# The last down projection of a two-layer diffusion backbone: its first two groups are loaded and split within the last up block, later weights load later, and the last four row tiles go in the order 0, 2, 1, 3

## The chip, the cores and the metric

The kernel runs on one core of a Trainium2 chip. The metric is device time in microseconds, from one launch to its end. A core has five engines that work side by side, each on a list of instructions of its own: PE (TensorE, matrix products), DVE (VectorE), ACT (ScalarE), POOL (GpSimd) and SP (SyncE, which here only issues transfers). PEld is PE's loading of a weight tile.

## The reference

Two layers over 1024 latent tokens of width 1024 and 256 context tokens. Each layer has a token mixer and then a gated feed-forward network with a convolution over positions. The change touches only the very last matrix product, `@ w_down` of the second layer:

```python
def conv_ffn(h, w_up, conv_w, conv_b, w_down):
    a, b = jnp.split(h @ w_up, 2, axis=-1)
    ap = jnp.pad(a, ((0, 0), (1, 1), (0, 0)))
    a = ap[:, :-2] * conv_w[0] + ap[:, 1:-1] * conv_w[1] + ap[:, 2:] * conv_w[2] + conv_b
    return (jax.nn.gelu(a) * b) @ w_down
...
x = x + g2 * rms_norm(conv_ffn(h, f_w_up[i], f_conv_w[i], f_conv_b[i], f_w_down[i]), norm_g[i, 3])
```

The hidden width is 2816, which is 22 blocks of 128. In the second layer only the latent tokens are needed, and `x` is the output.

## The kernel before

**Exact products from split numbers.** Each float32 operand is split in two: ACT casts it to a high part (`CAST`, tiles `ah` and `wh`), DVE subtracts to get the low part (`TENSOR_TENSOR`, tiles `al` and `wl`). A product is three matmuls: high by high, high by low, low by high. `split_into` does one split, so each 128x1024 operand costs one cast on ACT and one subtraction on DVE before PE can use it.

**The up projection.** `lat_ffn` walks over the 22 blocks of the hidden width. `up` makes one block with seven block products (a fast-multiplication scheme in the style of Strassen and Winograd) in the accumulators X, Y, Z (`psB`). Their weights come from the generator `weights`, advanced by `step(more)` inside the block before. The tiles `wh` and `wl` have four buffers each, and a block uses all four. `conv_gate` makes the gated activations, and `Q.dma_start(actd[...])` on SP writes them to memory (`actd`). `pair_sums` reads two blocks back and writes four combinations (`actc`).

**The down projection.** `down_blocks` does the same trick for the 1024x2816 by 2816x1024 product: seven products `p1`, `p6`, `p7`, `p4`, `p5`, `p3`, `p2`, each over 11 pairs of blocks, taken two pairs at a time as groups 0 to 5 (group 5 has one pair). A group is 24 matmuls (12 for group 5), so a product is 132. `fetch(p, g)` loads the activations (tile `raw`) and what it needs of the weights, and splits both. It runs up to three groups ahead of the matmuls. The weights come as four quarters: `r1` (quarter 11), `r12`, `r22`, and quarter 21, which is loaded where it is used. `p1` needs `r1` alone. `p6` needs `r12 - r1` (written over `r1`) and `r22` minus that. Before the change `fetch("p1", g)` loads `r1[g]`, `r12[g]` and, for the first three groups, `r22[g]`, each as two transfers of 256 KB on SP.

**The accumulators.** `p1` and `p2` accumulate in two tiles `psA` of two banks each: row tiles 0 and 1 share the first, 2 and 3 the second. After `p1`, ACT copies the four banks to `s1` (`after("p1")`). The products `p6`, `p7`, `p4` go to four `psB` tiles. At the end, the last three groups of `p2` are done row tile by row tile (15 matmuls each), and `final(t)` squares, gates, normalises, adds and stores that row tile.

**The order of the work.** The code's order is a wish: a scheduler in the framework places instructions by its own costs, and each engine then runs its list as it stands. A wait on a tile is a wait on the whole tile, both banks of a `psA` included. In the trace nearly all instructions carry L50, a helper's line, so they are told apart by their tiles.

Of the kernel before, what the change touches and what calls it, by code (L numbers as in the profile page):

```python
# [15 lines left out]
P = 128  # L16
# [16 lines left out]
def hybrid_kernel(  # L33
# [24 lines left out]
    Q = Engine(nc.sync, "Q")  # L58
# [32 lines left out]
    def t_row(dt=F32, shape=(P, 1024)):  # L91
        return sb.tile(list(shape), dt, name=nm("row"), tag="row", bufs=10)
# [848 lines left out]
    def lat_ffn(l, stage, n0, halos, gate, between, steady, ctx=None, after=None):  # L941
# [98 lines left out]
        def pair_sums(n, f0, f1):  # L1040
# [16 lines left out]
            yield  # L1057

        def run_late():
            while late:  # L1060
                late.pop(0)()

        def next_weights(nxt):
            W = ahead.pop("W")
            if nxt is None:
                return W, iter(())
            ahead["W"] = {}
            return W, weights(l, nxt[0], ahead["W"], nxt[1] in ("plain", "ctx"))
# [135 lines left out]
        for (f, how), nxt in zip(jobs, jobs[1:] + [None]):  # L1204
# [10 lines left out]
            n = made.index(f)  # L1215
# [4 lines left out]
        if ctx is None:  # L1220
            step(sums_, 9)
            down_blocks(l, stage, gate, pairs, pair_sums(len(pairs) - 1, *pairs[-1]))
            return
# [84 lines left out]

    def down_blocks(l, stage, gate, pairs, rest):
        open_pool("down%d" % l)  # L1310
# [8 lines left out]
        def kept(tag, n=1024):  # L1319
            return pool.tile([P, n], F32, name=nm(tag), tag=tag, bufs=1)  # L1320

        first = [(a_tile("h"), a_tile("l")) for _ in range(3)]
        r1 = [kept("r1%d" % g) for g in range(NG)]
        r12 = [kept("r12%d" % g) for g in range(NG)]
        ys = [kept("y%d" % t) for t in range(8)]
        s1 = [kept("s1%d" % i, n=512) for i in range(4)]
        r22 = [t_row() for _ in range(NG)]

# [4 lines left out]

        sides = {"p1": (0, 0), "p2": (1, 0), "p4": (1, 512)}
        kinds = {"p5": 0, "p6": 1, "p7": 2, "p3": 3}
        ready = {}

        def fetch(p, g):
            n = width[g]
            raw = t_raw()  # L1340
            if p in kinds:
                a = members[g][0]
                Q.dma_start(raw[:, 0:n].rearrange("p (k c) -> p k c", c=512),
                            actc[kinds[p], a:a + len(members[g])].rearrange("k p c -> p k c"))
            else:
                second, o = sides[p]
                for j, m in enumerate(members[g]):
                    Q.dma_start(raw[:, j * 512:(j + 1) * 512], actd[pairs[m][second], :, o:o + 512])
            if p == "p1":
                w_part(r1[g], g, 0, 0)  # L1350
                w_part(r12[g], g, 0, 1)
                if g < 3:
                    w_part(r22[g], g, 1, 1)
                src = r1[g]
            elif p == "p6":
                if g < 3:
                    w_part(r22[g + 3], g + 3, 1, 1)
                V.tensor_sub(r1[g][:, 0:n], r12[g][:, 0:n], r1[g][:, 0:n])
# [9 lines left out]
            else:  # L1368
                src = t_raw()
                w_part(src, g, 1, 0)  # L1370
                if p == "p4":
                    V.tensor_sub(src[:, 0:n], src[:, 0:n], r22[g][:, 0:n])
                    V.tensor_tensor(out=src[:, 0:n], in0=src[:, 0:n], in1=r1[g][:, 0:n], op=ALU.add)
            ops = []
            for x, tiles in ((raw, first.pop(0) if first else [a_tile(z) for z in "hl"]),
                             (src, [t_w("w" + z) for z in "hl"])):
                split_into([t[:, 0:n] for t in tiles], x[:, 0:n])
                ops.append(tiles)
            ready[p, g] = ops

# [105 lines left out]
        while got < len(todo):  # L1486
            fetch(*todo[got])
            got += 1
        for i in range(4):
            while chores:  # L1490
                chores.pop(0)()
            for p, g in tail:
                mms(A[i], p, g, list(range(len(members[g]))), i, False, g == NG - 1)
            final(i, A[i])
# [572 lines left out]
```

## Time and profile before

| what | value |
|---|---|
| median of 3 runs | 2918.66 us (2913.76 to 2921.04) |
| profiled execution, its own time | 2913.42 us |
| its span, first to last instruction | 2911.6 us |
| PE busy | 2775.0 us, 95% of the span |
| DVE, ACT, POOL busy | 72%, 47%, 23% |
| mean granted TensorE clock | 0.984 |
| transfers | 513.78 MB, mean 176 GB/s |

Times in the rows below are microseconds from the span's start. In a timeline a row is: start, duration, engine, line, operation, output tile <- inputs, shape, how many were merged; in brackets the idle time of that engine just before, and what ended it. In the chain of waits a row is: start, length, engine or transfer, and the chain follows from the last instruction back to whatever released it. In a table by stretch a row gives busy time and, after it, the granted clock, the share of DMA engines busy and GB/s.

### The profile page before, as it was taken

What the parts mean: (1) busy time and instruction counts of PE and PEld (TensorE: products, weight loads), DVE (VectorE), ACT (ScalarE), POOL (GpSimd) and SP (SyncE); (2) the same over time, 40 slices, a digit from 0 to 9 for tenths busy, and PEclk for the clock granted to TensorE, in tenths of its full rate; (3) what the DMA queues carried; (4) which work ended last, traced back from release to release, by engine and by line L of the source; (5) the groups of instructions that cost most, each with busy time, mean ns of one, the idle gap of its engine ahead of it and who ended that gap; (6) DMA issues with size and microseconds to landing.
All of it is one profiled execution on the core that took longest, in us unless ns stands there. A gap on an engine that the chain in (4) does not pass through costs nothing.

```text
span 2911.6 us, 40240 instructions
## 1 busy us (share of the span) xinstructions
PE 2775.0 (95%) x14702; PEld 2387.4 (82%) x14702; DVE 2108.0 (72%) x3175; ACT 1371.2 (47%) x2298; POOL 677.2 (23%) x1002
## 2 busy tenths in 40 slices
PE   7999999999999999999999999899997999999998
PEld 5798988999898888888877777888886988887787
DVE  6557675655787888778643669887886688887766
ACT  4332242323575445544324534777875444444433
POOL 1150130620201122220003025565552112220001
PEclk9999999999999999999999999999997999999999
DMA  7764356522575323546855865356575345445654
GB/s 258 238 193 147 115 176 217 170 89 80 191 231 176 112 98 121 161 159 213 298 168 175 280 206 185 113 172 228 184 237 178 116 156 184 149 145 182 231 170 156
DMA packets 418200, 513.78 MB, mean 176 GB/s; under 512 B 18641, under 2 KB 298065, under 8 KB 418001
## 3 DMA queue, kind: packets, MB, share of 16 engines
q1 hardware_dynamic: 361585, 448.01, 48.1%
q10 hardware_dynamic: 55264, 58.99, 6.0%
q0 software_dynamic: 1152, 4.19, 0.4%
q8 instruction: 116, 1.90, 0.3%
q14 instruction: 83, 0.68, 0.1%
HBM read 403.12 MB, written 108.00 MB: 176 GB/s over the span
## 4 chain that ended last, share of the span: by engine, by line
PE 50%; DMA 9%; DVE 6%; ACT 3%; issue 3%; POOL 2%; SPq 0%; ACTq 0%; DVEq 0%; POOLq 0%
PE psB L50 42%; PE psA L50 8%; DVE row L50 2%; DVE wl L50 2%; DMA raw<-in_f_w_up_dram 2%; DMA raw<-in_f_w_down_dram 2%; DMA raw<-actd 1%; ACT wh L50 1%; ACT row L50 1%; ACT tmp L50 1%; POOL sm L50 1%; DMA row<-xT 1%; DMA araw<-in_ada_w_dram 0%; DMA raw<-in_ada_w_dram 0%; ACT act L50 0%
## 5 line engine op out<-in xcount | busy, mean ns | idle before, releaser
L50 PE MATMUL psB<-cmb,wh 128*128 128x512 f32 (+2 forms) x2584 | 748.5, 374 | 4.7 <-ACT row L50 2.4
L50 ACT CAST wh<-raw 128x1024 fp32r<-128x1024 f32 (+1 forms) x376 | 331.8, 895 | 481.2 <-PE psB L50 177.9
L50 PEld LDWEIGHTS psB<-cmb,wh 128*128 128x128 f32 x2584 | 471.9, 188 | 94.1 <-ACT row L50 3.3
L50 PE MATMUL psB<-cmb,wl 128*128 128x512 f32 (+2 forms) x1292 | 482.8, 374 | 0.0
L50 DVE TENSOR_TENSOR wl<-raw,wh 128x1024 fp32r<-128x1024 f32 (+1 forms) x376 | 382.6, 1030 | 115.2 <-ACT wh L50 114.4
L50 PE MATMUL psB<-wh,big 128*128 128x512 f32 x864 | 285.8, 398 | 3.4 <-DVE row L50 2.0
L50 PEld LDWEIGHTS psB<-cmb,wl 128*128 128x128 f32 x1292 | 243.3, 188 | 43.4
L50 POOL TENSOR_SCALAR sm<-sm 128x1 f32<-128x1 f32 (+1 forms) x76 | 42.9, 565 | 938.6 <-ACT junk L50 382.1
L50 POOL TENSOR_TENSOR row<-raw,raw 128x512 f32<-128x512 f32 x44 | 74.9, 1702 | 593.9 <-DMA raw<-in_f_w_up_dram 435.1
L50 ACT CAST wh<-row 128x512 fp32r<-128x512 f32 (+1 forms) x150 | 118.1, 789 | 179.0 <-DVE row L50 93.7
L50 PE MATMUL psB<-wh,act 128*128 128x512 f32 x640 | 199.8, 390 | 1.6 <-DVE tmp L50 1.6
L50 PE MATMUL psA<-big,wh 128*128 128x320 f32 x1024 | 194.5, 312 | 2.9 <-ACT wh L50 1.7
L50 PEld LDWEIGHTS psB<-wh,big 128*128 128x128 f32 x864 | 163.9, 190 | 40.6 <-ACT big L50 2.4
L50 DVE SCALAR_TENSOR_TENSOR row<-row,cwcols,row 128x1024 f32<-128x1024 f32 (+2 forms) x142 | 151.0, 1064 | 37.2 <-ACT row L50 21.8
L50 ACT CAST ah<-raw 128x1024 fp32r<-128x1024 f32 (+1 forms) x79 | 79.7, 1011 | 198.2 <-PE psB L50 111.5
L50 PE MATMUL psB<-wl,big 128*128 128x512 f32 x432 | 167.3, 396 | 0.0
L50 PEld LDWEIGHTS psA<-big,wh 128*128 128x128 f32 x1024 | 160.8, 189 | 3.9 <-ACT wh L50 2.3
L50 DVE TENSOR_TENSOR al<-raw,ah 128x1024 fp32r<-128x1024 f32 (+1 forms) x79 | 92.6, 1174 | 95.0 <-ACT ah L50 94.8
L50 POOL TENSOR_SCALAR row<-row,sm,sm 128x128 f32<-128x128 f32 x160 | 120.9, 770 | 148.5 <-DMA row<-vscr 142.5
L50 PE MATMUL psB<-wh,al 128*128 128x512 f32 x388 | 151.2, 390 | 0.0
L50 PE MATMUL psB<-wh,ah 128*128 128x512 f32 x388 | 151.1, 390 | 0.0
L50 PE MATMUL psB<-wl,ah 128*128 128x512 f32 x388 | 151.1, 389 | 0.0
(275 smaller groups left out, 6212.0 us busy)
## 6 DMA issues: line engine op xcount, KB each, us to landing
raw<-in_f_w_up_dram SPq DMA_DIRECT2D x142, 512.0 KB, 4.7
raw<-in_a_w_in_dram SPq DMA_DIRECT2D x64, 512.0 KB, 4.8
raw<-in_ada_w_dram SPq DMA_DIRECT2D x64, 512.0 KB, 4.8
wh<-woscr SPq DMA_DIRECT2D x48, 512.0 KB, 4.7
raw<-actd SPq DMA_DIRECT2D x44, 512.0 KB, 4.7
actd<-row SPq DMA_DIRECT2D x39, 512.0 KB, 2.6
raw<-in_a_w_out_dram SPq DMA_DIRECT2D x35, 512.0 KB, 3.5
xT<-row ACTq DMA_DIRECT2D x33, 512.0 KB, 5.1
```

The lines of the kernel that those rows point to most:

```text
L50: ins = fn(*a, **kw)
```

## The change

It does four things.

- A generator `lead_in` runs within the last up block, where there are no more up weights to prepare. It loads the activations and the `r1` weights of groups 0 and 1 of `p1` (into tiles `raw` and `row`) and splits them into `wh` and `wl` tiles as these come free. `down_blocks` then takes them as ready, and the three early `a` tiles serve groups 2, 3 and 4.
- `r12` and `r22` are no longer loaded with `fetch("p1", g)`, but by a table `side_loads`, partly with the later groups of `p1` and partly with those of `p6`. The number of bytes stays the same.
- `r1[0]`, `r1[1]` live in `row` tiles and `r22[0]`, `r22[1]` in the stage's own pool, the other way round than before.
- The last four row tiles are taken in the order 0, 2, 1, 3 instead of 0, 1, 2, 3.

```diff
--- before.py
+++ after.py
@@ -1056,6 +1056,35 @@
             Q.dma_start(actc[2:4, n].rearrange("s p c -> p s c"), w.rearrange("p (s c) -> p s c", s=2))
             yield
 
+        early = {}
+
+        def lead_in():
+            def load(n):
+                raw = t_raw()
+                for j in range(2):
+                    Q.dma_start(raw[:, j * 512:(j + 1) * 512], actd[pairs[2 * n + j][0], :, 0:512])
+                return raw
+
+            def halves(src):
+                hl = [t_w("w" + z) for z in "hl"]
+                split_into(hl, src)
+                return hl
+
+            acts, early["b11"] = [], [t_row(), t_row()]
+            for n, w in enumerate(early["b11"]):
+                acts.append(load(n))
+                for j in range(2):
+                    f = pairs[2 * n + j][0]
+                    Q.dma_start(w[:, j * 512:(j + 1) * 512], w_down[l][f * P:(f + 1) * P, 0:512])
+            yield
+            early["act"] = [halves(acts[0])]
+            yield
+            early["w"] = [halves(early["b11"][0])]
+            yield
+            yield
+            early["act"].append(halves(acts[1]))
+            early["w"].append(halves(early["b11"][1]))
+
         def run_late():
             while late:
                 late.pop(0)()
@@ -1063,7 +1092,7 @@
         def next_weights(nxt):
             W = ahead.pop("W")
             if nxt is None:
-                return W, iter(())
+                return W, lead_in() if ctx is None else iter(())
             ahead["W"] = {}
             return W, weights(l, nxt[0], ahead["W"], nxt[1] in ("plain", "ctx"))
 
@@ -1219,7 +1248,7 @@
         run_late()
         if ctx is None:
             step(sums_, 9)
-            down_blocks(l, stage, gate, pairs, pair_sums(len(pairs) - 1, *pairs[-1]))
+            down_blocks(l, stage, gate, pairs, pair_sums(len(pairs) - 1, *pairs[-1]), early)
             return
         open_pool("down%d" % l)
         pool = stage_pool["pool"]
@@ -1306,7 +1335,7 @@
             step(extra, 99)
             ctx_down(l, stage, gate, chain(*[ada_cols(1, m, st, accs, True) for m, st, accs in sums]), after)
 
-    def down_blocks(l, stage, gate, pairs, rest):
+    def down_blocks(l, stage, gate, pairs, rest, early):
         open_pool("down%d" % l)
         pool = stage_pool["pool"]
         NP = len(pairs)
@@ -1320,11 +1349,11 @@
             return pool.tile([P, n], F32, name=nm(tag), tag=tag, bufs=1)
 
         first = [(a_tile("h"), a_tile("l")) for _ in range(3)]
-        r1 = [kept("r1%d" % g) for g in range(NG)]
+        r1 = early["b11"] + [kept("r1%d" % g) for g in range(2, NG)]
         r12 = [kept("r12%d" % g) for g in range(NG)]
         ys = [kept("y%d" % t) for t in range(8)]
         s1 = [kept("s1%d" % i, n=512) for i in range(4)]
-        r22 = [t_row() for _ in range(NG)]
+        r22 = [kept("r22%d" % g) for g in range(2)] + [t_row() for _ in range(2, NG)]
 
         def w_part(dst, g, second, h):
             for j, m in enumerate(members[g]):
@@ -1332,13 +1361,18 @@
                 Q.dma_start(dst[:, j * 512:(j + 1) * 512], w_down[l][f * P:(f + 1) * P, h * 512:(h + 1) * 512])
 
         sides = {"p1": (0, 0), "p2": (1, 0), "p4": (1, 512)}
+        side_loads = {("p1", 2): ((0, 0),), ("p1", 3): ((0, 1), (1, 0)), ("p1", 4): ((0, 2),), ("p1", 5): ((0, 3), (1, 1)),
+                      ("p6", 0): ((0, 4), (1, 2)), ("p6", 1): ((0, 5), (1, 3)), ("p6", 2): ((1, 4),), ("p6", 3): ((1, 5),)}
         kinds = {"p5": 0, "p6": 1, "p7": 2, "p3": 3}
         ready = {}
 
         def fetch(p, g):
             n = width[g]
-            raw = t_raw()
-            if p in kinds:
+            hl = early["act"][g] if p == "p1" and g < 2 else None
+            raw = None if hl else t_raw()
+            if hl:
+                pass
+            elif p in kinds:
                 a = members[g][0]
                 Q.dma_start(raw[:, 0:n].rearrange("p (k c) -> p k c", c=512),
                             actc[kinds[p], a:a + len(members[g])].rearrange("k p c -> p k c"))
@@ -1346,15 +1380,13 @@
                 second, o = sides[p]
                 for j, m in enumerate(members[g]):
                     Q.dma_start(raw[:, j * 512:(j + 1) * 512], actd[pairs[m][second], :, o:o + 512])
+            if p == "p1" and g > 1:
+                w_part(r1[g], g, 0, 0)
+            for second, m in side_loads.get((p, g), ()):
+                w_part((r12, r22)[second][m], m, second, 1)
             if p == "p1":
-                w_part(r1[g], g, 0, 0)
-                w_part(r12[g], g, 0, 1)
-                if g < 3:
-                    w_part(r22[g], g, 1, 1)
                 src = r1[g]
             elif p == "p6":
-                if g < 3:
-                    w_part(r22[g + 3], g + 3, 1, 1)
                 V.tensor_sub(r1[g][:, 0:n], r12[g][:, 0:n], r1[g][:, 0:n])
                 src = t_row()
                 V.tensor_sub(src[:, 0:n], r22[g][:, 0:n], r1[g][:, 0:n])
@@ -1371,12 +1403,15 @@
                 if p == "p4":
                     V.tensor_sub(src[:, 0:n], src[:, 0:n], r22[g][:, 0:n])
                     V.tensor_tensor(out=src[:, 0:n], in0=src[:, 0:n], in1=r1[g][:, 0:n], op=ALU.add)
-            ops = []
-            for x, tiles in ((raw, first.pop(0) if first else [a_tile(z) for z in "hl"]),
-                             (src, [t_w("w" + z) for z in "hl"])):
-                split_into([t[:, 0:n] for t in tiles], x[:, 0:n])
-                ops.append(tiles)
-            ready[p, g] = ops
+            if hl is None:
+                hl = first.pop(0) if first else [a_tile(z) for z in "hl"]
+                split_into([t[:, 0:n] for t in hl], raw[:, 0:n])
+            if p == "p1" and g < 2:
+                wl = early["w"][g]
+            else:
+                wl = [t_w("w" + z) for z in "hl"]
+                split_into([t[:, 0:n] for t in wl], src[:, 0:n])
+            ready[p, g] = hl, wl
 
         def mms(bank, p, g, js, i, first, last):
             (ah, al), (wh, wl) = ready[p, g]
@@ -1486,7 +1521,7 @@
         while got < len(todo):
             fetch(*todo[got])
             got += 1
-        for i in range(4):
+        for i in (0, 2, 1, 3):
             while chores:
                 chores.pop(0)()
             for p, g in tail:
```

How this moves instructions at three places:

**ACT, from the end of the last up block through p1.** `row_24825`/`row_24841` is the block's last copied accumulator. `r_4252` to `r_4254` are the weights `r1` of groups 0 to 2 before. After the change `row_24749`/`row_24750` are those of groups 0 and 1, and `r_4264` those of group 2. Before:

```order
L50 COPY row_24775<-psB_24747 128x2x256
L50 COPY row_24825<-psB_24746 128x2x256
L50 ACTIVATE row_24859<-row_24825,lncols,cwcols_734 128x1024
L50 CAST ah_24875<-raw_24913 128x1024
L50 CAST ah_24877<-raw_24928 128x1024
L50 CAST ah_24879<-raw_24943 128x1024
L50 CAST wh_24922<-r_4252_24881 128x1024
L50 ACTIVATE row_24859<-row_24859 128x1024
L50 CAST wh_24937<-r_4253_24882 128x1024
L50 CAST wh_24952<-r_4254_24883 128x1024
```

And now:

```order
L50 COPY s_24805<-psB_24748 128x512
L50 CAST wh_24845<-row_24749 128x1024
L50 COPY row_24787<-psB_24747 128x2x256
L50 COPY row_24841<-psB_24746 128x2x256
L50 CAST wh_24879<-raw_24756 128x1024
L50 CAST wh_24883<-row_24750 128x1024
L50 ACTIVATE row_24887<-row_24841,lncols,cwcols_734 128x1024
L50 CAST ah_24903<-raw_24939 128x1024
L50 CAST ah_24905<-raw_24983 128x1024
L50 CAST ah_24907<-raw_25025 128x1024
L50 CAST wh_24948<-r_4264_24909 128x1024
```

The casts of group 0 moved ahead of the block's last copies (that of its activations, `wh_24808`, is one row further up), and those of group 1 ahead of the convolution's `ACTIVATE`.

On SP in the same stretch, the weights `r1` of groups 3, 4 and 5 (`r_4265`, `r_4266`, `r_4267`) now stand so, with the gated activations of the last block stored by `actd<-row_24887`, read back by `row_24977<-actd`, and their sums stored to `actc`:

```order
L50 DMA r_4265_24910<-in_f_w_down_dram 128x512 x2
L50 DMA r_4269_24914<-in_f_w_down_dram 128x512
L50 DMA actd<-row_24887 128x1024
L50 DMA r_4269_24914<-in_f_w_down_dram 128x512
L50 DMA r_4286_24931<-in_f_w_down_dram 128x512 x2
L50 DMA row_24977<-actd 128x1024
L50 DMA r_4266_24911<-in_f_w_down_dram 128x512 x2
L50 DMA r_4270_24915<-in_f_w_down_dram 128x512 x2
L50 DMA raw_25064<-actd 128x512
L50 DMA actc<-row_24980 128x2x512
L50 DMA actc<-row_24981 128x2x512
L50 DMA r_4267_24912<-in_f_w_down_dram 128x512
```

Between two loads of `r1` there stood before one `r12` and one `r22` as well; now it is fewer weights, but the group 5 weights stand behind both stores of sums.

**ACT, from p1 to p6.** `psA_24911`/`psA_24937` holds row tiles 0 and 1 of `p1`, `psA_24912`/`psA_24938` row tiles 2 and 3. `ah_25115`, `wh_25117` (now `ah_25112`, `wh_25116`) are the operands of group 0 of `p6`. Before:

```order
L50 CAST wh_25078<-r_4257_24886 128x512
L50 CAST ah_25115<-raw_25108 128x1024
L50 CAST wh_25117<-row_25113 128x1024
L50 COPY s_4272_24901<-psA_24911 128x512
L50 COPY s_4273_24902<-psA_24911 128x512
L50 COPY s_4274_24903<-psA_24912 128x512
L50 CAST ah_25154<-raw_25147 128x1024
L50 COPY s_4275_24904<-psA_24912 128x512
```

And now:

```order
L50 CAST wh_25075<-r_4267_24912 128x512
L50 COPY s_4282_24927<-psA_24937 128x512
L50 COPY s_4283_24928<-psA_24937 128x512
L50 CAST ah_25112<-raw_25103 128x1024
L50 COPY s_4284_24929<-psA_24938 128x512
L50 CAST wh_25116<-row_25110 128x1024
L50 COPY s_4285_24930<-psA_24938 128x512
L50 CAST ah_25152<-raw_25144 128x1024
```

Both casts for `p6` stood ahead of the copies that end `p1`. Now the first stands behind two of the copies, the second behind three.

On DVE the low parts of that first group follow in this order now, with one more subtraction (`r_4266`) between them, which before was done earlier:

```order
L50 TENSOR_TENSOR row_25110<-r_4286_24931,row_24749 128x1024
L50 TENSOR_TENSOR al_25113<-raw_25103,ah_25112 128x1024
L50 TENSOR_TENSOR r_4266_24911<-r_4272_24917,r_4266_24911 128x1024
L50 TENSOR_TENSOR wl_25117<-row_25110,wh_25116 128x1024
L50 TENSOR_TENSOR row_25150<-r_4287_24932,row_24750 128x1024
```

**PE, the last four row tiles.** `psA_24911`/`psA_24937` holds row tiles 0 and 1, the other `psA` tiles 2 and 3; `wh_26335,ah_26333` opens a row tile, `wh_26401,al_26400` ends it. Before, the end of the second row tile taken up to the start of the last:

```order
L50 MATMUL psA_24912<-wh_26401,ah_26399 128x512
L50 MATMUL psA_24911<-wh_26335,ah_26333 128x512
...
L50 MATMUL psA_24911<-wh_26401,al_26400 128x512
L50 MATMUL psA_24912<-wl_26402,ah_26399 128x512
L50 MATMUL psA_24912<-wh_26401,al_26400 128x512
L50 MATMUL psA_24912<-wh_26335,ah_26333 128x512
```

And now:

```order
L50 MATMUL psA_24938<-wh_26403,ah_26399 128x512
L50 MATMUL psA_24938<-wl_26404,ah_26399 128x512
L50 MATMUL psA_24938<-wh_26403,al_26400 128x512
L50 MATMUL psA_24937<-wh_26337,ah_26333 128x512
...
L50 MATMUL psA_24937<-wh_26403,al_26400 128x512
L50 MATMUL psA_24938<-wh_26337,ah_26333 128x512
```

The scheduler had already put row tile 2 ahead of row tile 1, all but its last two matmuls; those stood right ahead of row tile 3. Now they stand 15 matmuls further up, and `final(2)` stands ahead of `final(1)` on ACT, DVE and POOL.

## The prediction, made before the changed kernel ran

> **What bounds the kernel now.** I read the shares of the engines first, then the chain of waits of the last 275 us, then PE's timeline where the chain leaves PE, and last ACT, DVE and SP at those places. The page gives PE 95% of the span, so a gain must come out of the places where PE stands still, or must shorten PE's own work, which this change does not. The chain, in order of time (start, length, what):
>
> ```profile
> 2636.49 41.71 PE psB L50 x192
> ...
> 2714.11 8.00 PE psA L50 x34
> 2722.11 29.92 PE psB L50 x132
> 2752.03 5.44 PE psA L50 x24
> ...
> 2888.14 9.79 PE psA L50 x43
> ...
> 2901.76 3.71 PE psA L50 x15
> 2905.49 0.60 ACT junk L50
> ```
>
> The up projection ends on PE at 2636.49 + 41.71 = 2678.20. The product `p6` begins at 2722.11, and its 132 matmuls take 29.92 us without a break. A group of 24 takes 5.44. `p1` has 132 matmuls too, but fills 2722.11 - 2678.20 = 43.91 us: **13.99 us of it are lost**. From `p6` on the chain lies on PE without a piece of another engine until the last row tiles. The second loss is between the end of the row tiles at 2897.9 and the last one at 2901.76. PE's timeline for the first (in brackets the idle time and its releaser):
>
> ```profile
> 2684.06 1.22 PE L50 MATMUL psA<-wh,ah 128*128 128x512 f32 x2 [5.88 <-ACT wh L50]
> 2686.26 0.80 PE L50 MATMUL psA<-wl,ah 128*128 128x512 f32 x1 [0.98 <-DVE wl L50]
> 2688.14 0.63 PE L50 MATMUL psA<-wh,al 128*128 128x512 f32 x1
> ...
> 2706.54 0.50 PE L50 MATMUL psA<-wl,ah 128*128 128x512 f32 x1 [0.65 <-DVE wl L50]
> ...
> 2712.85 0.73 PE L50 MATMUL psA<-wh,ah 128*128 128x512 f32 x2 [0.99 <-ACT wh L50]
> 2714.11 0.50 PE L50 MATMUL psA<-wl,ah 128*128 128x512 f32 x1 [0.53 <-DVE wl L50]
> ```
>
> Group 0 waits for its split: 5.88 + 0.98. Groups 3 and 4 wait for loads and splits: 0.65 + 0.99 + 0.53 = 2.17. Between them the matmuls themselves are slow. The table by short stretches shows why (length, PE busy, then the granted clock):
>
> ```profile
> 2681.00:2681.50 0.50, 0.00 (x0) 1.00 0.92 348
> 2681.50:2682.00 0.50, 0.00 (x0) 0.78 1.05 389
> ...
> 2691.50:2692.00 0.50, 0.50 (x3) 0.50 0.82 168
> 2692.00:2692.50 0.50, 0.50 (x4) 0.98 0.56 160
> ...
> 2898.30:2901.70 3.40, 0.07 (x1) 1.00 0.11 43
> 2901.70:2905.00 3.30, 3.24 (x14) 1.00 0.73 273
> ```
>
> The clock fell to half about 3.5 us after the last matmul and stayed there until 2692, while the gap of 3.4 us at the end left it at 1.00. [...]
>
> **The change part by part. 1: the early groups.** ACT takes its list in order, and group 0's weights stood at its end:
>
> ```profile
> 2680.14 2.92 ACT L50 CAST ah<-raw 128x1024 fp32r<-128x1024 f32 x3
> 2682.97 1.04 ACT L50 CAST wh<-r 128x1024 fp32r<-128x1024 f32 x1
> ```
>
> Now four casts of 1.04 and four subtractions of 1.22 (row below) stand within the last block or right at its end. Each needs a `wh` buffer that the block still uses. Its seven products are 12 matmuls each (2.7 us, half a group), and buffers come free after products 2, 4, 6 and 7; these rows date two of them:
>
> ```profile
> 2669.98 0.58 ACT L50 COPY row<-psB 128x512 f32<-128x512 f32 x1 [2.13 <-PE psB L50]
> 2675.50 0.69 DVE L50 TENSOR_TENSOR row<-psB,row 128x512 f32<-128x512 f32 x1 [2.88 <-PE psB L50]
> ```
>
> Product 4 is done at 2669.95, so group 0's weights are cast by 2671.0 and subtracted by 2672.3, 6 us early. Product 6 is done at 2675.5: group 1's activations by 2677.8. Product 7 at 2678.20: group 1's weights by 2678.2 + 1.05 on ACT and, after two additions on DVE, by about 2681. Group 1 is due at 2678.20 + 5.44 = 2683.64. In the block the extra work is covered by ACT's and DVE's idle time (2.13 and 2.88 in these rows); a copy is moved back by 1.04, two products ahead of the matmul that needs its bank. If that cover were gone, it would cost at most 1 us. So PE goes from the last block to `p1` without a wait and at full clock: all 13.99 are on offer.
>
> **2: groups 2 to 5 in p1.** Group 2's weights are issued when a `raw` buffer is free (2677.8) and have until 2689.1. For groups 4 and 5 it is close. Rows of `r` tiles (issue in ns, landing), and of transfers:
>
> ```profile
> L50 SPq DMA_DIRECT2D r<-in_f_w_down_dram x22: 328/430/902, 2673.1 to 2709.3; - x22
> ...
> DMA to landing us min/median/max: 3.7/5.9/7.2
> ```
>
> ```profile
> 2687.37 0.33 SPq L50 DMA_DIRECT2D actd<-row  x1
> ```
>
> ```profile
> row<-actd SPq DMA_DIRECT2D x4, 512.0 KB, 6.2
> actd<-row SPq DMA_DIRECT2D x2, 512.0 KB, 2.9
> ```
>
> The store waits for the same convolution chain, so it stays at about 2687.4; its read-back goes out at 2690.3, and group 4's `r1` behind it by 2691.2. Landing at 5.9 is 2697.1, cast and subtraction 1.04 + 1.22, with DVE's four sums for the last pair (0.6 each) ahead of the latter: 2700.3 at worst against a due time of 2678.20 + 4 x 5.44 = 2699.96. Group 5 stands behind those sums and both stores: the read-back lands at 2696.5, sums by 2699, issue 2700, landing by 3.7 to 5.9 later, split 1.3: 2705.0 to 2707.2, against 2705.4. The bounds are nothing and the 2.17 that groups 3 and 4 pay now. Since fewer transfers share the engines in this stretch, I take the lower side: **-0.8**.
>
> **3: a new wait between p1 and p6.** This is what the order shows and the description does not. Before, both casts for group 0 of `p6` ran ahead of the copies of `p1`'s banks; these rows are ACT, then DVE:
>
> ```profile
> 2717.61 1.05 ACT L50 CAST ah<-raw 128x1024 fp32r<-128x1024 f32 x1 [1.40 <-DMA raw<-actc]
> 2718.57 1.04 ACT L50 CAST wh<-row 128x1024 fp32r<-128x1024 f32 x1
> 2720.79 1.07 ACT L50 COPY s<-psA 128x512 f32<-128x512 f32 x2 [1.18 <-PE psA L50]
> 2722.15 0.59 ACT L50 COPY s<-psA 128x512 f32<-128x512 f32 x1 [0.28 <-PE psA L50]
> ```
>
> ```profile
> 2718.70 1.23 DVE L50 TENSOR_TENSOR al<-raw,ah 128x1024 fp32r<-128x1024 f32 x1
> 2719.84 1.22 DVE L50 TENSOR_TENSOR wl<-row,wh 128x1024 fp32r<-128x1024 f32 x1
> ```
>
> The copies waited for PE and began 1.2 us before the end of `p1` (call that T = 2721.95, when the first matmul of `p6` starts). Now the list has two copies first, so ACT reaches the cast of `ah` at about T - 0.2, ends it at T + 0.85, does the third copy until T + 1.3 and the cast of `wh` until T + 2.3. DVE then has `al`, one subtraction (`r_4266`) and `wl` at 1.135 each (2719.84 - 2718.70 is 1.14): from T + 0.87 to T + 4.4. PE can do four matmuls (0.91) on `wh` from T + 2.3, then waits for `wl` until T + 4.4: lost 4.4 - 0.9 = **-3.5**. Its bounds are 2.3, were `wl` not late, and 8.7, the 6.9 of group 0's old wait with the slow clock's first half. I take the worked value since each link has its row.
>
> **4: later loads of r12 and r22.** Same transfers, same bytes. In `p6` a group takes 5.44 and DVE's work for it, four subtractions at 1.14 at most, 4.6. The second group is due at T + 3.5 + 5.44, and its `wl` comes, by the list, at T + 8.5; later ones have more room. Zero, between 0 and -1.
>
> **5: the order 0, 2, 1, 3.**
>
> ```profile
> 2893.29 0.68 DVE L50 TENSOR_TENSOR y<-psA,gate 128x512 f32<-128x512 f32 x1
> ...
> 2898.54 0.59 ACT L50 ACTIVATE junk<-psA 128x512 bf16<-128x512 f32 x1
> ...
> 2901.03 0.68 DVE L50 TENSOR_TENSOR y<-psA,gate 128x512 f32<-128x512 f32 x1
> ...
> 2901.76 0.50 PE L50 MATMUL psA<-wh,ah 128*128 128x512 f32 x1 [3.39 <-DVE y L50]
> ```
>
> Row tile 3 shares a tile with 2, so it waited until 2's gating had read it, and that stood behind row tile 1's. Now tile 2 is complete 15 matmuls earlier, at about 2895; its square and gating (0.7 + 0.7) end by 2896.5, before row tile 3 is due at 2898.2. Row tile 1 must follow tile 0's reading, done at 2893.97, and starts at 2894.8. The gap closes: 2901.76 - 2898.21 = **+3.55**. Behind the last matmul nothing changes: the end was and is one row tile's `final`. If `final(1)` were late, at most 1.4 of DVE work would stand in the way.
>
> **Sum:** 13.99 - 0.8 - 3.5 + 0 + 3.55 = 13.24 us. Against the profiled execution (2913.42) that gives 2900.2. That execution lies 5.24 under the median of the runs; from the median, 2918.66 - 13.24 = **2905.4**, which I predict.
>
> **The rivals.** A difference under 0.3% (8.8 us, a border at 2909.9) is about what these measurements cannot tell from no change.
>
> - *No new wait at p6.* ACT gets to the casts in time: +3.5, 2901.9. It needs ACT to pass a copy that waits, which no row shows; ACT's casts waited behind others in each row above. [...]
> - *The clock halves at p6.* [...] Price: before, some 17 matmuls at 0.43 instead of 0.227, 3.4 us: 2908.8.
> - *The loads still hold p1.* Groups 2 to 5 go on losing what lies beyond group 0: 13.99 - 5.88 - 0.98 - 3.4 = 3.7, or, if one wait passes 3.5 us, 3.4 more. 2908.3 to 2911.7, say 2910. For it: SP stops for the store and the sums with `r1` of groups 4 and 5 behind; against it: less traffic.
> - *The early splits come no earlier.* If group 0's loads landed only after the block, the head would keep its waits and pay p6's too; the tail and groups 3 and 4 remain: about +2, 2916.5. The loads go out near 2660 and need 7.2 at most, product 4 ends at 2669.95: unlikely.
> - *Slower: p6 waits for each of its loads.* If `r12[g]` and `r22[g]` arrived only when PE asks, a group would take a landing, two subtractions, a cast and another subtraction, 7.2 + 2.4 + 1.0 + 1.2 = 11.8 instead of 5.44. Past two such groups the gain is gone; five and a half make +35 and 2940. Against it: `fetch` runs three groups ahead, and 1.5 MB per group need about 4 us at the 389 GB/s of the row above.
>
> **How the numbers follow.** Forecast 0.55 (its own range 2900 to 2909, by the spread of the runs and step 2 and 3's bounds), no new wait 0.09, half clock 0.08, loads 0.19, no earlier 0.06, slower 0.03. The range from 2896 (no new wait, at the profiled run's level) to 2913 (the loads' upper end and a little) leaves out under 2 in 10. Faster by over 0.3%: 0.95 of the forecast, the first two rivals nearly whole, half of the loads: 0.77. Slower by as much 0.04, the rest 0.19.
>
> **What would show it.** Right: PE at full clock and without a wait from the last block into `p1`; under 1 us idle at its groups 4 and 5; then two waits at the first group of `p6`, some 2.3 on ACT's `wh` and 1.2 on DVE's `wl`; no gap before row tile 3, and 3.5 us less from the first matmul of the last four to the end. Wrong: a half-clock stretch anywhere after 2678, long ACT waits for `r` loads in `p1`, DVE named before later groups of `p6`, or a gap in the last up block.

## The result: faster by 13.7 us, 0.5%, with a wait where one was forecast, but dearer

| kernel | median of the runs | ratio to before, 95% interval |
|---|---|---|
| before | 2916.72 us (6 runs, 2913.76 to 2923.26) | |
| after | 2903.01 us (6 runs, 2896.91 to 2905.92) | 0.9948, 0.9932 to 0.9963 |
| after, a second time | 2901.85 us (5 runs; before 2915.40, 9 runs) | 0.9952, 0.9939 to 0.9966 |

The forecast was 2905.4. The chain of waits of the changed kernel, from the last part of the up projection on (start, length, what):

```profile
2629.95 38.76 PE psB L50 x179
...
2696.43 6.80 DMA raw<-actc
2705.85 2.07 PE psB L50 x4
2707.95 31.30 PE psB L50 x128
2739.25 5.44 PE psA L50 x24
...
2815.41 59.91 PE psB L50 x264
2875.32 13.63 PE psA L50 x60
```

Two things are gone: `p1` no longer shows as waits and pieces, and the last 60 matmuls are one piece, where the chain before had 43, a gap and 15. One thing is new: a transfer, `raw<-actc`, stands ahead of `p6`, whose 132 matmuls now take 2.07 + 31.30 = 33.4 us instead of 29.92. PE's timeline at these places:

```profile
2671.25 0.39 PE L50 MATMUL psB<-cmb,wl 128*128 128x512 f32 x1
2671.48 0.39 PE L50 MATMUL psA<-wh,wh 128*128 128x512 f32 x1
...
2701.53 0.39 PE L50 MATMUL psA<-wh,al 128*128 128x512 f32 x1
2705.85 2.07 PE L50 MATMUL psB<-wh,ah 128*128 128x512 f32 x4 [3.93 <-ACT wh L50]
2707.95 0.79 PE L50 MATMUL psB<-wl,ah 128*128 128x512 f32 x1
```

`p1` begins 0.23 us after the up projection's last matmul, with operands that both lie in `wh` tiles (the early splits), and runs through. Then PE stands still for 3.93 us. That is its only wait down to the end, as the list of PE's waits says (total, times, longest). Before, the same stretch has 12.4 us in six waits: 5.88, 0.98, 0.65, 0.99, 0.53 and 3.39. After:

```profile
PE psB L50 <- ACT wh L50: 3.9, 1, 3.9
```

ACT and SP at the seam of `p1` and `p6`, after:

```profile
2700.59 1.08 ACT L50 COPY s<-psA 128x512 f32<-128x512 f32 x2 [2.90 <-PE psA L50]
2703.32 1.04 ACT L50 CAST ah<-raw 128x1024 fp32r<-128x1024 f32 x1 [1.65 <-DMA raw<-actc]
2704.27 0.58 ACT L50 COPY s<-psA 128x512 f32<-128x512 f32 x1
2704.75 1.05 ACT L50 CAST wh<-row 128x1024 fp32r<-128x1024 f32 x1
```

```profile
2687.24 0.38 SPq L50 DMA_DIRECT2D raw<-actd  x1
2691.80 1.09 SPq L50 DMA_DIRECT2D actc<-row  x2
2692.94 3.38 SPq L50 DMA_DIRECT2D r<-in_f_w_down_dram  x5
2696.43 0.38 SPq L50 DMA_DIRECT2D raw<-actc  x1
```

The order on ACT is the one that the prediction read: copies, `ah`, copy, `wh`. But ACT also stood 1.65 us until `raw` had landed. SP issued that transfer only at 2696.43, behind two stores to `actc` and five pieces of `r` weights. The queue had stood from 2687.62 until 2691.80, when DVE had the sums that the first of these stores writes. The clock at this place (stretch, its length, PE busy, granted clock, DMA share, GB/s):

```profile
2705.00:2705.50 0.50, 0.00 (x0) 0.89 1.07 414
2705.50:2706.00 0.50, 0.15 (x1) 0.50 1.05 406
2711.50:2712.00 0.50, 0.50 (x3) 0.50 1.14 393
2712.00:2712.50 0.50, 0.50 (x3) 0.78 0.78 213
2712.50:2713.00 0.50, 0.50 (x3) 1.00 0.78 254
```

It stood at 0.50 from 2705.4 to 2712.2, so `p6` began at half speed, with 0.43 us from one matmul to the next instead of 0.227.

**A yardstick for what follows.** In these two profiles the up projection's last matmul starts at 2671.25 after and at 2677.79 before:

```profile
2677.79 0.39 PE L50 MATMUL psB<-cmb,wl 128*128 128x512 f32 x1
```

So 6.54 of the 16.51 us between the two profiled executions (2913.42 and 2896.91) were there when the up projection ended; the experiments ask whether by chance. They did not arise in the last up block, where the early splits run: its 84 matmuls take 18.96 us from the first start to the last in both profiles, and in every other one of this document. The change itself is read from the stretch "to the end": 2911.6 - 2677.79 = 233.81 before, 2895.1 - 2671.25 = 223.85 after, **9.96 us** less. I split it in four: the head (that last matmul to `p6`'s first), `p6`'s 132 matmuls, the middle, and the tail (first matmul of the last row tiles to the end).

| kernel | `p6`'s first raw tile, ACT's order there | head | p6 | tail | to the end |
|---|---|---|---|---|---|
| before | in time, casts first | 44.16 | 29.92 | 23.62 | 233.81 |
| after | late, copies first | 34.60 | 33.24 | 19.94 | 223.85 |
| after, again | late, copies first | 33.28 | 31.79 | 19.96 | 221.12 |
| order alone, two runs | in time, casts first | 43.56, 43.86 | 29.92 | 19.95, 19.94 | 229.56, 229.84 |
| head alone | late, copies first | 34.88 | 33.00 | 25.28 | 229.30 |
| early splits, old loads, two runs | in time, casts first | 37.40, 38.51 | 29.92 | 20.00, 19.99 | 223.40, 224.53 |
| later loads, no early splits | in time, `wh` behind one copy | 41.26 | 30.42 | 20.00 | 227.82 |
| filler matmuls | late, copies first | 34.48 | 31.24 | 20.50 | 222.93 |
| casts first | late, casts first | 35.40 | 32.87 | 20.02 | 224.42 |
| early raw, copies first | early, copies first | 34.08 | 31.32 | 20.17 | 221.69 |
| **early raw, two runs** | early, casts first | 30.34, 31.57 | 29.92 | 19.99, 19.94 | **216.38, 217.56** |

The middle is 136.1 in all of them but the one with filler matmuls (136.7).

### The profile page after: what moved, and what is told of

It reads as the page before. It is cut to its first block, busy times and chain, and to the rows that moved or that the text cites. A ratio compares the mean times of both kernels' runs of the same rounds, so it can differ in the third digit from the quotient of the medians.

```text
span 2895.1 us, 40248 instructions
## 1 busy us (share of the span) xinstructions
PE 2765.4 (96%) x14702; PEld 2379.7 (82%) x14702; DVE 2112.9 (73%) x3175; ACT 1371.5 (47%) x2298; POOL 676.2 (23%) x1002
```

## The experiments

### The parts of the change, one by one

**The order of the row tiles alone** (the kernel before with one edit):

```diff
-        for i in range(4):
+        for i in (0, 2, 1, 3):
```

> The kernel before with the order 0, 2, 1, 3 alone. Theory: the tail is a matter of the order only. From the first matmul of the last row tiles to the end of the span takes 19.8 us (19.78 after, 23.46 before), no idle of PE over 0.5 us ahead of the last 15 matmuls; the stretch from the last matmul of the up projection (its start) to the first of p6 stays at 44.3 us as before. Rival: the tail became shorter because of what the other parts do (weights in other tiles), then it stays near 23.5 us here. Second question, for the 6.5 us by which the changed kernel's profiled execution already leads when the up projection ends: if that is chance, the up projection's last matmul here starts somewhere between 2671 and 2684 us; if the lead comes from the early loads, it starts within 1 us of 2677.8 here.

Measured: tail 19.95 against 23.62, head 43.56 with all of its waits. The order alone makes the tail's 3.67 us. Time 2908.3 beside 2917.32 (one run each).

**The change without the new order:**

```diff
-        for i in (0, 2, 1, 3):
+        for i in range(4):
```

> The changed kernel with the last row tiles back in the order 0, 1, 2, 3. Theory: the head is as in the changed kernel, 34.6 us from the start of the up projection's last matmul to p6's first (44.3 before) and p6's first 132 matmuls at 33.4 us (29.9 before), and the tail is back at 23.5 us, with an idle stretch of some 3.4 us ahead of the last 15 matmuls. Rival: as for the tail alone, then the tail stays near 19.8 us. If the lead upstream comes from the early loads, the up projection's last matmul starts near 2671.3 us again; if by chance, anywhere between 2671 and 2684.

The head is as after (34.88; one wait of 0.34 in `p1`). The gap is back, but the tail takes 25.28, 1.66 more than before with the same gap. PE's timeline has the gap, and the stretches behind it the reason:

```profile
2891.99 0.50 PE L50 MATMUL psA<-wh,ah 128*128 128x512 f32 x1 [3.39 <-DVE y L50]
```

```profile
2891.50:2892.00 0.50, 0.01 (x1) 1.00 0.93 348
2892.00:2892.50 0.50, 0.50 (x2) 0.92 1.05 389
2892.50:2893.00 0.50, 0.50 (x2) 0.50 0.83 311
...
2896.00:2897.00 1.00, 1.00 (x6) 1.00 0.00 0
```

Through an idle stretch of 3.39 us the clock stayed at 1.00 in the kernel before, and here it fell to 0.50 behind one of the same length. So the new order is worth 3.7 us, or 5.3 where the clock falls. Time 2905.26 beside 2917.32.

**Early splits, but r12 and r22 loaded as before:**

```diff
-        side_loads = {("p1", 2): ((0, 0),), ("p1", 3): ((0, 1), (1, 0)), ...
+        side_loads = {("p1", g): ((0, g),) + (((1, g),) if g < 3 else ()) for g in range(NG)}
+        side_loads.update({("p6", g): ((1, g + 3),) for g in range(3)})
```

> The changed kernel with r12 and r22 loaded with p1's groups as before: early splits without the later loads. Theory A (the early splits bring the gain, the later loads keep it): groups 2 to 5 of p1 and p6's first raw tile now stand behind 3 more pieces (r12 of groups 4 and 5, r22 of group 2, 1.25 MB, 3.3 us at the 380 GB/s of this stretch), so p1 waits 1 to 4 us at groups 2 to 5 and the stretch from the up projection's last matmul to p6's first grows from 34.6 to 36 to 40 us. Theory B (the loads fit under the up block or p1 anyway): the stretch stays within 1 us of 34.6.

> Early splits with r12 and r22 at their old places again, now timed. Theory A (the later loads only move the wait: with them it is ahead of p6, without them in p1): to the end 223.4 us as in the first look, and a time like the changed kernel's, 11 to 15 us under before. Theory B (the later loads are part of the gain): over 4 us slower than the changed kernel, less than 9 us under before.

PE's waits, first of its two profiles:

```profile
PE psA L50 <- ACT wh L50: 4.8, 1, 4.8
```

The wait is in `p1` now, at group 2, whose `r` tile stands behind 2 MB of side loads and a store to `actc` (its second half behind one to `actd` as well), and the clock stands at 0.50 there for 6.83 us; `p6` has none. Its raw tile lands 3.9 and 4.8 us before `p1` ends, and ACT's list has both casts ahead of the copies. The head grows by 2.8 (37.40) or 3.9 (38.51) over the first profile after, inside the range of theory A, and `p6` falls back to 29.92. To the end it is 223.40 and 224.53, against 223.85 and 221.12. Time 2901.68 beside 2917.32 at first (one run each), then 2903.20 (6 runs), ratio 0.9968 (0.9955 to 0.9980), an interval that overlaps with that of the changed kernel. So the later loads do free `p1`; what they save there is spent again ahead of `p6`.

**Later loads and the new order, no early splits** (`lead_in` is left out, and all groups load and split as before):

> The order 0, 2, 1, 3 and the later loads of r12 and r22, without the early loads and splits. Theory A: p1's loss was group 0's split, which stays: the 5.9 us wait for group 0's weights, some 1.0 for their low part and the slow matmuls behind them stay (about 10 of 13.99 us), and only the 2.2 us of groups 3 and 4 can go; the stretch from the up projection's last matmul to p6's first is 41 to 44.3 us against 44.3 before and 34.6 after. Theory B (p1 was held by the number of bytes in flight, so that loading r12 and r22 later frees it): the stretch falls under 39 us.

The wait of 5.88 and the 0.98 behind it are still there, those of groups 3 and 4 are gone. Head 41.26, 2.90 less than before: theory A. Without the early splits the head keeps most of its loss. Time 2909.45 beside 2917.32 (one run each).

### What holds p6

**The changed kernel again, and with filler matmuls.** The second puts 12 matmuls that nothing uses between `p1` and `p6`:

```diff
+            if p == "p6" and g == 0:
+                (dh, _), (dw, _) = ready["p1", NG - 1]
+                for _ in range(12):
+                    tc.keep_in_program_order(T.matmul(B[0][3], dh[:, 0:P], dw[:, 0:512], start=True, stop=True, ...))
```

> The changed kernel once more, unaltered, in the company of the next three. Theory: from the start of the up projection's last matmul to the end of the span 223.9 us (223.85 in its first profile, 233.81 before), with 3.9 us idle ahead of p6 and half clock behind. Of the median difference of 13.7 us only these 10 belong to the down projection; the rest is the up projection's end, 6.5 us earlier in the first profile. If that is chance, it shows here anywhere from 0 to 7; if it belongs to the change, again some 6 to 7 us (up projection's last matmul near 2671).

> The changed kernel with 12 matmuls more between p1 and p6 (p1's last operands, into a bank that p6 then starts afresh), 2.7 us of PE work in a gap of 3.9 us; they compute nothing that is used. Theory A (3.5 us of the loss at p6 are the half clock behind the gap): p6 starts as late as in the changed kernel, 34.6 us after the up projection's last matmul, its four first matmuls then wait for wl until about 2.1 us after its start, but its 132 matmuls take 31.0 us at most instead of 33.2 (29.9 at full clock and without that wait); the stretch to the end falls from 223.9 to 221.5. Theory B (the matmuls behind the gap are slow for another reason, the transfers' traffic for one): p6 stays at 33.2 us.

The changed kernel again: the wait was 2.97, with `raw` only 0.69 late for ACT instead of 1.65, and the clock was down for one stretch of 3.41 us instead of 6.83. So its head and `p6` vary with when a transfer lands. With the fillers, PE's stretches read:

```profile
2711.80:2714.70 2.90, 2.88 (x13) 1.00 1.04 398
2714.70:2715.20 0.50, 0.00 (x0) 1.00 1.06 410
2715.20:2717.70 2.50, 1.55 (x6) 1.00 1.05 402
```

The clock stays at 1.00, `p6` takes 31.24 instead of 33.24, and 0.9 us of wait for `wl` comes back that the slow matmuls had covered. Theory A, though 0.2 us over its bound of 31.0: the slow stretch is the clock, not traffic (402 GB/s here too). As a remedy it is poor: 0.9 us less than the first profile to the end, 1.8 more than the second, since the head stays and 0.6 us of small waits came in later. Time 2900.78 (5 runs), ratio 0.9960 (0.9946 to 0.9974).

**Casts ahead of the copies, loads unchanged:**

```diff
+            pin = (p, g) == ("p6", 0)
+            if pin:
+                pins.add("S")
...
-                    S.copy(s1[i], A[i])
+                    tc.keep_in_program_order(S.copy(s1[i], A[i]))
```

> The changed kernel with ACT's casts for p6's groups 0 and 1 ahead of the four copies of p1's banks, the loads left where they are. Theory A (the raw tile's landing is the limit): ah is cast at 2703.3 + 1.0 as before, wh right behind it, p6 starts at most 0.5 us earlier, about 34.1 us after the up projection's last matmul, and the clock halves all the same: 223 to 224 us to the end. Theory B (as in the prediction: ACT's order holds p6): p6 starts 3 us earlier, the clock stays up, and the stretch to the end falls by 4 to 7 us.

ACT's rows:

```profile
2712.53 1.04 ACT L50 CAST ah<-raw 128x1024 fp32r<-128x1024 f32 x1 [5.60 <-DMA raw<-actc]
2713.49 1.04 ACT L50 CAST wh<-row 128x1024 fp32r<-128x1024 f32 x1
```

ACT stood ready for 5.60 us. The raw tile landed 1.4 us after `p1` had ended (2711.16), both casts had to follow, and PE waited 3.42. That is 0.5 less than the first time, as theory A has it, though the 224.42 to the end lie above its 223 to 224; the head is 35.40, with 1.10 of small waits in `p1`. The theory of the prediction, that ACT's order holds `p6`, falls in this form: with the loads as they are, the wait is there without it. Time 2902.38 (5 runs), ratio 0.9955 (0.9942 to 0.9969).

**The raw tile early, with the loads of r12[3] and r22[1] behind it:**

```diff
-... ("p1", 4): ((0, 2),), ("p1", 5): ((0, 3), (1, 1)),
-                      ("p6", 0): ((0, 4), (1, 2)), ("p6", 1): ((0, 5), (1, 3)), ("p6", 2): ((1, 4),), ("p6", 3): ((1, 5),)}
+... ("p1", 4): ((0, 2),),
+                      ("p6", 0): ((1, 1), (0, 3)), ("p6", 1): ((1, 2), (0, 4)), ("p6", 2): ((1, 3), (0, 5)),
+                      ("p6", 3): ((1, 4),), ("p6", 4): ((1, 5),)}
```

> The changed kernel with r12[3] and r22[1] (four transfers, 1 MB) issued behind the raw tile of p6's group 0, and the later loads shifted accordingly; in the scheduler's order ACT's casts for that group then also stand ahead of the copies. Theory A (p6 waits because its raw tile is issued late on SP and lands at 2703.2, behind that 1 MB, 2.7 us at 380 GB/s): the raw tile lands about 2.6 us earlier, both casts are done when p1 ends, p6 starts 30.4 to 31.5 us after the up projection's last matmul instead of 34.6 and takes 29.9 to 32 us instead of 33.2, since the clock stays up; the stretch to the end is 216.5 to 219 us against 223.9. Theory B (the transfer engines are full, and the loads held back now make p6's group 1 wait as long): the stretch stays at 222 to 224 us, with an idle place at p6's second group.

> The early raw tile again, unaltered. Theory: again no wait of PE from the up projection's last matmul to the end, which takes 216.4 us (216.0 to 217). In time 3 to 7 us less than the changed kernel, so 14 to 21 us less than before; if the up projection's end varies by chance, its last matmul starts anywhere between 2671 and 2681 us.

SP, then ACT, first run:

```profile
2692.26 0.38 SPq L50 DMA_DIRECT2D actc<-row  x1
2692.69 0.46 SPq L50 DMA_DIRECT2D r<-in_f_w_down_dram  x1
2693.24 0.79 SPq L50 DMA_DIRECT2D raw<-actc  x1
2695.13 0.37 SPq L50 DMA_DIRECT2D actc<-row  x1
```

```profile
2697.14 1.04 ACT L50 CAST wh<-row 128x1024 fp32r<-128x1024 f32 x1
2699.41 1.05 ACT L50 CAST ah<-raw 128x1024 fp32r<-128x1024 f32 x1 [1.22 <-DMA raw<-actc]
2701.50 1.08 ACT L50 COPY s<-psA 128x512 f32<-128x512 f32 x2 [1.04 <-PE psA L50]
```

The transfer now stands behind one store instead of two, and one piece of weights instead of five. Counted from the up projection's last matmul (2672.32 here) it goes out at 20.9 us instead of 25.2, and `ah` is cast at 27.1 instead of 32.1. Both casts end before `p1` does. ACT's list changed with the edit, both casts now standing ahead of the copies; the next run parts the two. The chain is nothing but matmuls:

```profile
2672.71 30.11 PE psA L50 x132
2702.83 29.92 PE psB L50 x132
...
2868.87 13.63 PE psA L50 x60
```

To the end 216.38; in the second run 217.56, over the 217 expected, with one wait of 1.13 in `p1`'s group 4. That is 17.4 and 16.3 us under before. Timed: 2898.16 (5 runs), ratio 0.9938 (0.9923 to 0.9952), and 2896.56 (6 runs), ratio 0.9939 (0.9923 to 0.9954). Over eleven runs each, on two occasions each, the mean is 2896.1 against 2901.4 of the changed kernel. The intervals of the ratios still overlap; the traces don't: 216.4 to 217.6 against 221.1 to 223.9. This is the best version found.

The edit brought a third thing forward, on DVE. In the changed kernel the weights for group 0 of `p6`, which `wh` is cast from, come as the second of these rows:

```profile
2700.72 1.23 DVE L50 TENSOR_TENSOR r<-r,r 128x1024 f32<-128x1024 f32 x1 [2.29 <-DMA r<-in_f_w_down_dram]
2701.86 1.22 DVE L50 TENSOR_TENSOR row<-r,row 128x1024 f32<-128x1024 f32 x1
```

By the code and the time of landing (2700.62), the first is group 3's `r12 - r1`, and it waits for r12[3], one of the five pieces ahead of the raw tile. So the weights were done at 2703.08, only 0.24 us before ACT took up the raw tile, and as close with the casts first (2712.29 against 2712.53). With the early raw tile this subtraction starts at 2692.15. An estimate from these rows: had the raw tile and the casts been early and r12[3] not moved, `wh` would have been ready at 2703.08 + 1.04, some 2.2 us after the end of `p1`. No run tried that.

**The raw tile early, but ACT's list at the seam as in the changed kernel** (copy, copy, `ah`, copy, `wh`, copy; the splits of `p6`'s groups 0 and 1 are written between and behind the copies, and ACT is kept to that order):

The part of the edit at the copies:

```diff
                 if p == "p1":
+                    pins.add("S")
                     S.copy(s1[i], A[i])
+                    for _ in range((0, 1, 1, 2)[i]):
+                        split_into(*behind.pop(0))
+                    pins.discard("S")
```

> The kernel with the early raw tile (r12[3] and r22[1] behind it), but with ACT's list at the seam of p1 and p6 in the changed kernel's order: copy, copy, ah, copy, wh, copy. Theory A (ACT's order alone costs what the prediction worked out, and in the changed kernel it was hidden behind the late raw tile): p6 starts 2.3 to 2.5 us after p1's end, then waits 1.0 to 1.4 us for wl; from the start of the up projection's last matmul to p6's first 32.7 us instead of 30.34 with the casts first, p6 31 us, to the end 219.5 to 220.5 us against 216.4 (up to 223 if the clock halves). Theory B (with the raw tile early, ACT's order does not matter): 216.4 to 217.

PE's waits:

```profile
PE psB L50 <- ACT wh L50: 2.2, 1, 2.2
PE psA L50 <- DVE wl L50: 1.3, 1, 1.3
PE psB L50 <- DVE wl L50: 0.9, 1, 0.9
```

2.18 for `wh`, then 0.95 for `wl` at `p6`: what the prediction had worked out for this order, 2.3 and 1.2. Without the 1.28 in `p1`, the head is 34.08 - 1.28 - 30.34 = 2.46 longer than with the casts first, and `p6` 31.32 - 29.92 = 1.40: 3.9 us in all, at full clock. To the end it is 221.69, or 220.4 without that 1.28. Theory A holds; ACT's order does cost this once the raw tile is no longer late. Time 2902.44 (6 runs), ratio 0.9957 (0.9946 to 0.9969).

### The lead ahead of the change

> The order 0, 2, 1, 3 alone again, now timed. Theory A (what the changed kernel gained ahead of the up projection's end is chance of the runs): 229.6 us to the end as in the first look, and a time 3 to 5 us under before. Theory B (the kernel before is slow upstream too for a reason that the change removes): the time gained here is the same, so it does not tell; but then the lead at the up projection's end is missing here, as it stays in every run with the early splits (last matmul under 2675 there, over 2677 here).

The order alone, again: 2908.67 (11 runs), ratio 0.9983 (0.9974 to 0.9992), that is 5.0 us under before (6.2 by the medians), and 4.0 us less to the end. The up projection's last matmul started at 2673.86, under the 2677 that theory B asked for. Over all profiles it starts at 2677.79, 2676.94, 2679.88 and 2673.86 in the four without early loads, and between 2671.25 and 2683.84, on average 2676.3, in the ten with them. The two sets overlap, PE's and DVE's instructions come in the same order up to the last up block, and that block takes 18.96 us in all fourteen. So the 6.54 us are chance of the two profiled executions. Why that point varies by 12 us was not studied.

## Why the prediction was right, and which terms were off

The forecast, 13.24 us under the median, met the time: 13.7 and 13.55 by the medians. By the trace the change is worth less, 9.96 and 12.69 us. The interval of the second comparison (0.9939 to 0.9966, that is 9.9 to 17.8 us) holds both, that of the first (10.8 to 19.8) only the larger. The forecast's closeness is in part luck: the new wait cost more than its term, and the medians hold a gain that the stretch to the end does not show. One of the prediction's own signs of being wrong, a half-clock stretch behind the up projection, did appear. Step by step:

- **Step 1, 13.99 on offer from the early splits: right.** With the seam's wait removed as well the head is 30.34, 13.82 less than before, and PE goes from the up projection into `p1` at full clock. With the later loads but without the early splits only 2.90 came.
- **Step 2, -0.8 for groups 2 to 5 of p1: within its bounds.** It was 0 in both profiles of the changed kernel and in one with the early raw tile, and 0.22 to 1.28 in the five others with early splits and later loads, mostly at group 4.
- **Step 3, -3.5 for the new wait at p6: the mis-sized term.** Against the 30.34 and 29.92 of the early raw tile, the changed kernel lost 4.26 + 3.32 = 7.6 us there, and 2.94 + 1.87 = 4.8 the second time. The mechanism exists, and its price was near where it stood alone (2.18 and 0.95, 3.9 in all). But in the changed kernel the late raw tile, with the weights 0.24 us ahead of it, was enough to hold `p6`: 3.42 with the casts first. Two things were left out. First, the step took ACT to be free to cast `ah` as soon as it reached it. But `raw` landed 1.65 and 0.69 us later; 2.3 + 1.65 and 2.3 + 0.69 are the waits measured, 3.93 and 2.97. The prediction listed the loads of groups 4 and 5 behind SP's stores, and didn't follow the queue one entry further, to `p6`'s own raw tile. Second, with both waits the clock fell to 0.50, for 6.83 and 3.41 us, and `p6` took 3.3 and 1.9 us more. With the clock at 1.00 `wl` took 0.9 (with the fillers) and 0.95 (copies first) instead.
- **Step 4, nothing for the later loads: right only as a sum.** They remove a wait of 4.4 to 4.8 us and a half-clock stretch of 6.83 from `p1`, and the new wait at `p6` takes as much.
- **Step 5, 3.55 from the order: right**, 3.68 in the first profile and 3.67 alone.

Of the rivals, "the clock halves at p6" did happen, at 0.08 the most underrated: it came with one wait of 3.93 or 2.97 us, while with waits of 2.18 and 0.95 one behind the other (copies first) the clock stayed at 1.00. "No new wait" is the version with the early raw tile, and it gave 2896 to 2898 instead of 2901.9. "The loads still hold p1" came true only with the old loads. The early splits did come early (`p1` starts 0.23 us behind the last block's last matmul), and the slower case showed nowhere.

## What to carry to other kernels

When a stall is taken out by work moved earlier, follow each queue past the moved part to the first load of the next phase: here 4.8 and 7.6 us of the 13.8 that the head had to give were lost again at `p6`, with its raw tile behind stores and weights that nobody needed yet, and its casts behind copies. When several causes end at nearly the same instant, removing one alone shows little (casts first: 0.5 us less wait; early raw tile with copies first: still 2.2), and only together does the wait go. Compare runs by a stretch that starts where the change starts; the time ahead of it moved more here than the change's last terms.

## What the runs showed of the hardware

In these traces the half clock came in whole stretches. Read from the granted clock, between the up projection and the last matmul it lasted 3.41 us (the changed kernel again, and the tail of the head alone), 6.83 (the changed kernel, the head alone, the casts first, both runs with old loads) or 10.24 (before, the order alone, no early splits), that is once, twice or three times 3.413 (10.24 / 3). The stretches at full clock between are whole multiples too: after, it runs from 2712.22 to 2893.12, 180.9 us or 53 times 3.413, though PE was busy nearly throughout.

The prediction read one fall of the clock about 3.5 us after a last matmul, and one gap of 3.4 us that left it at 1.00. In the kernel with old loads less was enough: PE stopped at 2687.77, yet the clock fell at 2689.9, only 2.1 us later, so that the 3.41 us before the fall held some 1.3 us of matmuls:

```profile
2689.50:2690.00 0.50, 0.00 (x0) 0.89 0.71 254
2690.00:2690.50 0.50, 0.00 (x0) 0.50 0.72 279
2696.50:2697.00 0.50, 0.50 (x3) 0.78 1.05 406
2697.00:2697.50 0.50, 0.50 (x4) 1.00 1.07 410
```

So a gap's length alone did not say here whether the clock falls: it fell with gaps of 2.97 and 3.42, not with one of 2.18, and with one of the two of 3.39 at the tail. Counted in steps of 3.413 us from the nearest change of the clock, the tail's gap before lies across two steps, 1.87 and 1.52 us of it; in the head alone 2.98 us of it lie in one. Whether this is what decides was not shown. The step that took the tail's gap of 3.4 us as harmless read one case of the two. A stretch of 3.41 us at half speed costs a busy PE 1.6 us by an estimate from the pitches before, 8 matmuls at 0.43 us (from 2687.3 to 2691.6) instead of 0.227 (from 2692.7); `p6` took 1.87 more in the second profile. In the down projection the clock fell with every gap of 2.97 us or more but one, the 3.39 before.
